# Narrow and wide expert turns interleaved in a two-layer decoder trunk, with another order of the layers' tasks

## The chip, the cores and the metric

The kernel runs on one NeuronCore of a Trainium2 chip. The metric is the device time of one execution in microseconds (us). TensorE is written PE here, VectorE DVE, ScalarE ACT, GpSimd POOL, SyncE SP; SP issues the loads.

## What is computed

The reference is a decoder trunk of two layers on 256 tokens of width 1024, in float32. Each layer has four mixer branches (S5, Mamba-2, retention, RG-LRU) merged by gates, a cross-attention on 256 memory tokens, and a feed-forward part. That part is a dense SwiGLU in layer 0 and eight experts in layer 1, of which each token takes two:

```python
def moe_swiglu(x, w_router, w1, w3, w2):
    logits = (t @ w_router).astype(jnp.float32)
    top_v, top_i = lax.top_k(logits, TOP_K)
    top_w = jax.nn.softmax(top_v, axis=-1)
    combine = jnp.einsum('tk,tke->te', top_w, jax.nn.one_hot(top_i, N_EXPERTS))
    out = combine[:, 0:1] * swiglu(t, w1[0], w3[0], w2[0])
    for e in range(1, N_EXPERTS):
        out = out + combine[:, e:e + 1] * swiglu(t, w1[e], w3[e], w2[e])
```

An expert has w1 and w3 of 1024 x 3584 and w2 of 3584 x 1024; the eight together are 352 MB of float32. A final RMSNorm ends the trunk.

## The kernel before

**The two layers.** Each projection is a `Job`: its weights come in loads of 512 KB, ACT and DVE split each into a high and a low float32r part (`whi`, `wlo`), and PE multiplies. Norms, scans, softmax and evacuations run as generators in lanes of the class `Loom`, which keeps a clock for each engine while the program is being written out and places a stage of a lane between two matmuls once it holds it to be ready. The table `ORDER` lists jobs and spawned tasks of both layers in the order in which they are written out (`0xa` is layer 0's cross-attention, `0xo0` a job of its output projection, `0ret` its retention). `LANES` holds two numbers for each lane: how early before its ready time a stage may be placed, and how far DVE and ACT may be behind. Each engine runs its instructions in the order written, so a matmul whose operand is late holds up everything behind it on PE.

**The experts** (`Trunk.experts`). The router counts the tokens of each expert, and `route` sorts the experts by count, the fullest first. There are eight turns; turn 0 is expert 0, and the number of the expert for each other turn is read from the sorted list when its loads are issued. A turn has a fixed number of places for tokens: the first five have 96 (`CP`), the last three 64 (`C0`). If an expert has more tokens than places, `overflow` runs the experts again for the rest.

A turn has seven blocks of 512 hidden columns. `up` multiplies eight loads (w1 and w3 side by side, `moe_w13`), `down` four (`moe_w2`); that is 12 loads of 512 KB, 84 for a turn and 672 in all. These weights are not split: PE multiplies raw float32. The matmuls for the first 64 places (`mm1`, 64 columns of the array for each half) and those for the other 32 (`mm2`, 32 columns for each quarter) are two passes over the same loads; a 64-place turn has only the first. The order is up(0), up(1), down(0), up(2), down(1) and so on across turns, so that `down` of a turn's last block stands behind `up` of the next turn's first.

`gather` picks the tokens of a turn (or of two turns at once, from turn 2 on) by matmuls with a 0/1 matrix `eg` into `xg`; it is started at a turn's fifth block for the next. `scatter` takes a finished turn back: ACT copies the sums from `py` to `ey` and rounds them to `eyh`, DVE makes the rest `eyl`, PE multiplies both by `eg`, and DVE adds the result into `h`.

**Loads.** SP issues them in the order of use. A load needs a free tile: 15 of three pools (`RAW`, `WHI`, `WLO`) and about 20 of the general pool (`rawm`), so some 35 loads, or 18 MB, may be ahead. A tile comes free when the last pass over it has run. `Stream.load` reckons with 1.43 ns for each element of a partition when it advances the clock of the loads.

Of the kernel before, what the change touches and what calls it, by code (L numbers as in the profile page):

```python
# [28 lines left out]
FF = 2816  # L29
FE = 3584  # L30
NE = 8
NB, CP, C0 = 5, 96, 64
AHEAD = 1
W1, W2, W3, W4 = 8, 4, 9, 4
SEC = dict(u=0, z=512, xbc=1024, dt=1792, q=1800, k=2312, v=2824, g=3336, xl=3848, gl=4360, gate=4872)
# [9 lines left out]


ORDER = """
0lru setup 0norm 0ret 0gl 0x 0run 0bc 0g 0ssd 0q 0build 0dt 0v 0u 0g1a 0g3b 0g3a 0z 0b3a 0b3b 0g1b 0b1a 0xa 0k 0g2a
0g2b 0mem 1run 0g0a 0glu 0b2a 0merge 0b1b 0g0b 0b2b 0xnorm 0b0b 0b0a 0K1 1build 0outa 0outb 0K0 0xq0 0V0 0xq1 1mem
0fnorm 0V1 1norm 0xo0 0xo1 1K1 0ffn 1lru 1K0 1x 1mem' 1ssd 1v 1dt 1bc 1ret 1u 1g3b 1gl 1xa 1q 1g3a 1k 1b3a 1b3b 1g  # L50
1g2b 1z 1g2a 1b2b 1g1b 1g1a 1b2a 1g0a 1merge 1b1a 1b1b 1g0b 1xnorm 1glu 1b0a 1b0b early 1outa 1outb 1V0 1xq0 1xq1 1V1
efnorm 1xo0 1xo1
"""


# [86 lines left out]
class Loom:  # L142
# [1 line left out]

    LANES = dict(norm=(0.2, 22.06), evac=(0.6, 1046.56), s5=(0.0, 3.12), q=(0.4, 3.12), a=(0.2, 2.0), b=(0.2, 3.12))

    BUSY = 5.5

# [118 lines left out]
class Stream:  # L269
# [12 lines left out]
    def load(self):  # L282
        k = self.k
        while len(self.loaded) < len(self.flat):
            j, (k0, nk) = self.flat[len(self.loaded)]
            w = j.w() if callable(j.w) else j.w
            src = w[k0 * P:(k0 + nk) * P, j.c0:j.c0 + j.n]

            pools = dict(raw=(k.wr, RAW))
            if j.raw and self.done >= self.parted:  # L290
                pools.update(whi=(k.wh, WHI), wlo=(k.wl, WLO))
            own = next((n for n, (_, bufs) in pools.items() if self.used[n] < bufs), None)
            if own:
                t = pools[own][0].tile([P, 1024], F32, tag=own, name=k.name("raw"))
                self.used[own] += 1
            elif k.loom.tiles + k.loom.want >= self.cap:
                break
            else:
                t = k.m("rawm")
            t = t[:, :nk * j.n]  # L300
            k.loom.clk["dma"] = max(k.loom.clk["dma"], k.loom.now) + nk * j.n * 1.43e-3
            k.nc.sync.eng.dma_start(t.rearrange("p (k n) -> p k n", k=nk), src.rearrange("(k p) n -> p k n", p=P))
            self.loaded.append((t, k.loom.clk["dma"] + 2.0, own))

# [111 lines left out]
class Trunk:  # L416
# [1373 lines left out]
    def moe(self, l, events):  # L1790
# [67 lines left out]

        def route():
            mp = self.cst  # L1860
            bef = self.m("bef")[:, 0:64].rearrange("p (i o) -> p i o", i=NE)
            nc.sync.dma_start(bef, a["before"].partition_broadcast(P))
            yield job.out
            sel, comb, slot = (mp.tile([P, 2, NE], F32, name=n) for n in ("sel2", "comb", "slot"))
            st.slot, st.comb, lg = slot, comb, st.lg.rearrange("p (t e) -> p t e", t=2)
# [37 lines left out]
            nc.vector.tensor_tensor(eq, eq, bef, op=ALU.mult)  # L1903
            nc.vector.tensor_tensor(oh, oh, eq, op=ALU.add)
            nc.vector.tensor_reduce(rk, oh, axis=AX.X, op=ALU.add)
            nc.vector.tensor_scalar(rk, rk, 1.0, None, op0=ALU.add)

            up = self.iota[:, 0:NE]
            nc.vector.tensor_tensor(oh, rk[:, None, :].to_broadcast(sh), up[:, :, None].to_broadcast(sh), op=ALU.is_equal)
            nc.vector.tensor_tensor(eq, oh, up[:, None, :].to_broadcast(sh), op=ALU.mult)  # L1910
            nc.vector.tensor_reduce(num, eq, axis=AX.X, op=ALU.add)
            nc.vector.tensor_scalar(num, num, -1.0, None, op0=ALU.add)
# [25 lines left out]

            yield 20.0
            last = sp[:, 0:2 * NE].rearrange("p (t e) -> p t e", t=2)  # L1940
            nc.vector.tensor_copy(last[:, :, :NB], st.slots[:, :, :NB])
            nc.vector.tensor_scalar(last[:, :, NB:], st.slots[:, :, NB:], CP / C0, None, op0=ALU.mult)
            ps = yield from self.bank()
            nc.tensor.transpose(ps[:2 * NE, 0:P], sp[:, 0:2 * NE], self.ident)
            yield
# [20 lines left out]
    def experts(self, st):  # L1966
# [7 lines left out]
        gathered = [[Event(), Event()] for _ in range(NE)]  # L1974
        done = [Event(), Event()]
        turns = [(0,), (1,), (2, 3), (4, 5), (6, 7)]
        cap = lambda e: CP if e < NB else C0

        def places(e):
            b_.xg.append(self.m(f"xg{e}").rearrange("p (d s) -> p d s", d=8))  # L1980
# [10 lines left out]
        def gather(es):  # L1991
# [5 lines left out]
                    places(e)  # L1997
            if es[0]:
                yield st.ordered
            i0, cp = es[0] % 4, cap(es[0])  # L2000
            G = b_.G[:, i0:i0 + n, :].rearrange("p i (t s) -> p i t s", t=2)
            for t in range(2):
                for i, e in enumerate(es):
# [30 lines left out]
        def scatter(e, py, halves, done=None):  # L2034
            S = b_.G[:, e % 4, :]
            if not b_.y:
                yield from self.room(3)
                b_.y += [self.m("ey"), self.m("eyh", F32R), self.m("eyl", F32R)]
                nc.gpsimd.memset(b_.y[0][CP:], 0.0)
            if e == NB:  # L2040
                nc.gpsimd.memset(b_.y[0][C0:CP], 0.0)
            y, yh, yl = b_.y
            yield st.weighted

            for c in halves:
                nc.scalar.copy(y[:C0, c * 512:c * 512 + 512], py[0][c * C0:c * C0 + C0, :])
                for q in range(2 * c, 2 * c + 2) if e < NB else ():
                    nc.scalar.copy(y[C0:CP, q * 256:q * 256 + 256], py[1][q * 32:q * 32 + 32, 0:256])
            o = slice(halves[0] * 512, halves[-1] * 512 + 512)
            if halves[-1]:  # L2050
                self.drop(len(py))
            yield
            nc.scalar.copy(yh[:, o], y[:, o])
            yield
            nc.vector.tensor_tensor(yl[:, o], y[:, o], f(yh)[:, o], op=ALU.subtract)
            yield
            for t in range(2):
                for c in halves:
                    o = slice(c * 512, c * 512 + 512)
                    ps = yield from self.bank()  # L2060
                    mm(ps, S[:, t * P:t * P + P], yh[:, o], start=True, stop=False)
                    mm(ps, S[:, t * P:t * P + P], yl[:, o], start=False, stop=True)
                    yield
                    hc = self.h[:, t, o]
                    nc.vector.scalar_tensor_tensor(hc, ps, st.comb[:, t, e:e + 1], hc, op0=ALU.mult, op1=ALU.add)
                    self.drop()
            if done:
                lm.signal(done)
# [10 lines left out]
        def up(e, b):  # L2079
# [13 lines left out]

            def ev(acc):
                nc.scalar.activation(t()[:, 0:256], acc[0][:, 0:256], AF.Silu)
                if e < NB:
                    nc.scalar.activation(t()[:, 256:384], acc[1][:, 0:128], AF.Silu)
                yield
                nc.vector.tensor_tensor(t()[:, 0:256], t()[:, 0:256], acc[0][:, 256:512], op=ALU.mult)
                if e < NB:  # L2100
                    nc.vector.tensor_tensor(t()[:, 256:384], t()[:, 256:384], acc[1][:, 128:256], op=ALU.mult)
                yield

                pt = yield from self.bank()
                n = 3 if e < NB else 2
                for j in range(n):
                    nc.tensor.transpose(pt[:, j * P:j * P + P], t()[:, j * P:j * P + P], self.ident)
                yield
                nc.vector.tensor_copy(b_.h[i][:, :n * P], pt[:, :n * P])
                self.drop()  # L2110

            need = lambda k: (gathered[e][k // 4],)
            j = Job(lambda: a["moe_w13"][turn(e), b], 0, 1024, 8, 1 + (e < NB), mm1, ev, need)
            j.raw = True
            if e < NB:
                j.more = mm2
            return j

        def down(e, b, done, py):
            def start():  # L2120
                if not py:
                    n = 1 + (e < NB)
                    lm.until(lambda: lm.side >= n)
                    lm.side -= n
                    py.extend(self.sidep.tile([P, 512], F32, tag="side", name=self.name("py")) for _ in range(n))
# [16 lines left out]
            jw = dict(need=lambda k: (done,), start=start)  # L2142
            if e < NE - 1 or b < nb - 1:
                jobs = [Job(w, 0, 1024, 4, 0, mm1, **jw)]
                if e < NB:
                    jobs[0].more, jobs[0].front = mm2, True
            else:
                jobs = [Job(w, c * 512, 512, 4, 0, lambda *x, c=c: mm1(*x, halves=(c,)), **jw) for c in range(2)]
# [22 lines left out]
    def overflow(self, st):  # L2171

        nc, raw = self.nc, self.raw
        last = raw.values_load(st.most[0:1, 0:1], min_val=0, max_val=2 * T)
        st.again = True
        for n in (CP, 2 * CP):
            with self.tc.If(last > n):
                nc.vector.tensor_scalar(st.slots[:, :, :NB], st.slots[:, :, :NB], float(CP), None, op0=ALU.subtract)
                nc.vector.tensor_scalar(st.slots[:, :, NB:], st.slots[:, :, NB:], float(C0), None, op0=ALU.subtract)
                self.stream(self.experts(st), more=True)  # L2180


# [94 lines left out]
def layout(inp):  # L2277
# [37 lines left out]
    for i, nm in enumerate(("lru_wa", "lru_wx")):  # L2315
# [8 lines left out]
                                 g["norm_final"][None, :]], axis=0),  # L2324
        "pp": z, "lam": np.stack(lam, axis=1).transpose(2, 1, 0, 3).reshape(P, -1), "s5bc": np.stack(s5, axis=3), "lruw": lw.reshape(NL, P, 2, 4, P),
        "kst": kst, "decay": decay, "freq": freq,
        "before": np.tril(np.ones((NE, NE), np.float32), -1)[None],
        **{n: g[n] for n in ("w_in", "b_gate", "s5_w_glu", "w_branch", "w_out", "xa_wq", "xa_wk", "xa_wv", "xa_wo",
                             "ffn_w1", "ffn_w3", "ffn_w2")},
        "moe_router": g["moe_router"][0], "moe_w2": g["moe_w2"][0],  # L2330
# [19 lines left out]
```

## Time and profile before

| | |
|---|---|
| median of 3 runs | 2095.37 us (2089.89 to 2096.30) |
| the profiled execution, its own time | 2091.97 us |
| its span, first to last instruction | 2090.1 us |
| busy: PE, DVE, ACT, POOL | 1984.1, 952.5, 648.0, 135.9 us |
| mean granted PE clock, as a share of 2.4 GHz | 0.974 |
| moved from HBM | 535.57 MB, 257 GB/s over the span |

The page divides the span into 40 slices of 52 us. PE is at nine tenths or more in most, and lower in the first, in two early ones and in the last three. The memory traffic is different: 122 to 263 GB/s in the two layers (to slice 22), 315 to 394 in slices 23 to 34, and 409 without change in slices 36 to 39. The chain that ended last is 79% PE and 9% DMA.

### The profile page before, as it was taken

What the parts mean: (1) busy time and instruction counts of PE and PEld (TensorE: products, weight loads), DVE (VectorE), ACT (ScalarE), POOL (GpSimd) and SP (SyncE); (2) the same over time, 40 slices, a digit from 0 to 9 for tenths busy, and PEclk for the clock granted to TensorE, in tenths of its full rate; (3) what the DMA queues carried; (4) which work ended last, traced back from release to release, by engine and by line L of the source; (5) the groups of instructions that cost most, each with busy time, mean ns of one, the idle gap of its engine ahead of it and who ended that gap; (6) DMA issues with size and microseconds to landing.
All of it is one profiled execution on the core that took longest, in us unless ns stands there. A gap on an engine that the chain in (4) does not pass through costs nothing.

```text
span 2090.1 us, 33394 instructions
## 1 busy us (share of the span) xinstructions
PE 1984.1 (95%) x12937; PEld 1275.4 (61%) x12937; DVE 952.5 (46%) x1750; ACT 648.0 (31%) x1041; POOL 135.9 (7%) x282
## 2 busy tenths in 40 slices
PE   7999889999999999999999999999999999999885
PEld 7878677898888998887798344434434343333211
DVE  5888988857555689788655101111010100110102
ACT  4755434545444484444453001010010000010001
POOL 6840005000000000000000000000000000000000
PEclk9999899999999999999999999999999999999998
DMA  6544345546665555445746989988989899999994
GB/s 224 166 141 137 122 134 169 177 145 213 185 193 185 183 179 153 149 125 174 263 161 240 386 345 370 352 346 315 394 315 352 332 371 394 402 409 409 409 409 188
DMA packets 194434, 539.00 MB, mean 258 GB/s; under 512 B 18442, under 2 KB 23562, under 8 KB 194258
## 3 DMA queue, kind: packets, MB, share of 16 engines
q1 hardware_dynamic: 194258, 536.69, 70.9%
q8 instruction: 106, 1.74, 0.3%
q14 instruction: 70, 0.57, 0.1%
HBM read 535.57 MB, written 1.05 MB: 257 GB/s over the span
## 4 chain that ended last, share of the span: by engine, by line
PE 79%; DMA 9%; DVE 4%; POOL 3%; ACT 2%; issue 1%; SPq 0%; DVEq 0%; ACTq 0%; POOLq 0%
PE acc L132 59%; PE py L132 10%; PE ps L132 10%; DMA rawm<-moe_w 5%; DMA raw<-moe_w 2%; DVE wlo L132 1%; POOL tbt L132 1%; ACT ey L132 1%; POOL scr L132 1%; DMA s5z<-s5bc 1%; DVE s5z L132 0%; ACT whi L132 0%; DVE s5s L132 0%; POOL sp_e L132 0%; DVE eyl L132 0%
## 5 line engine op out<-in xcount | busy, mean ns | idle before, releaser
L132 DVE TENSOR_TENSOR wlo<-raw,whi 128x1024 fp32r<-128x1024 f32 (+2 forms) x311 | 372.3, 1215 | 118.0 <-PE acc L132 60.9
L132 ACT ACTIVATE whi<-raw 128x1024 fp32r<-128x1024 f32 (+2 forms) x311 | 322.4, 1052 | 225.0 <-PE acc L132 177.7
L132 DVE TENSOR_TENSOR eht<-eht,acc 128x256 f32<-128x256 f32 x91 | 33.7, 370 | 667.4 <-ACT eht L132 667.4
L132 PE MATMUL acc<-rawm,xg 128*32 128x256 f32 (+1 forms) x2308 | 321.3, 482 | 6.3 <-DMA rawm<-moe_w 6.2
L132 ACT ACTIVATE eht<-acc 128x256 f32<-128x256 f32 x91 | 31.2, 343 | 758.1 <-PE acc L132 758.1
L132 PE MATMUL acc<-whi,xh 128*128 128x512 f32 (+1 forms) x640 | 254.8, 398 | 0.1
L132 PE MATMUL acc<-wlo,xh 128*128 128x512 f32 (+1 forms) x640 | 247.2, 386 | 3.4 <-DVE wlo L132 3.3
L132 PE MATMUL acc<-whi,xl 128*128 128x512 f32 (+1 forms) x640 | 246.6, 385 | 0.0
L132 PE MATMUL acc<-raw,xg 128*32 128x256 f32 (+1 forms) x1724 | 239.0, 479 | 4.0 <-DMA raw<-moe_w 3.8
L132 PEld LDWEIGHTS acc<-rawm,xg 128*32 128x32 f32 (+1 forms) x2308 | 109.1, 122 | 199.0 <-issue 129.0
L132 PE MATMUL acc<-xh,whi 128*128 128x256 f32 (+1 forms) x632 | 181.9, 288 | 1.4 <-ACT whi L132 1.2
L132 PE MATMUL acc<-xh,wlo 128*128 128x256 f32 (+1 forms) x632 | 179.5, 284 | 3.6 <-DVE wlo L132 3.6
L132 PE MATMUL acc<-xl,whi 128*128 128x256 f32 (+1 forms) x632 | 179.6, 284 | 0.6 <-DVE xl L132 0.4
L132 PE MATMUL py<-rawm,eh 128*32 128x256 f32 (+1 forms) x1140 | 165.7, 478 | 4.2 <-DMA rawm<-moe_w 4.1
L132 PEld LDWEIGHTS acc<-raw,xg 128*32 128x32 f32 (+1 forms) x1724 | 82.1, 122 | 142.5 <-issue 88.9
L132 PEld LDWEIGHTS acc<-whi,xh 128*128 128x128 f32 x640 | 120.7, 189 | 28.6 <-issue 5.7
L132 PEld LDWEIGHTS acc<-wlo,xh 128*128 128x128 f32 x640 | 120.7, 189 | 26.5 <-DVE wlo L132 5.1
L132 PEld LDWEIGHTS acc<-whi,xl 128*128 128x128 f32 x640 | 120.6, 188 | 24.3 <-DVE xl L132 0.2
L132 PE MATMUL py<-raw,eh 128*32 128x256 f32 (+1 forms) x876 | 126.0, 477 | 1.2 <-DMA raw<-moe_w 1.2
L132 PEld LDWEIGHTS acc<-xh,wlo 128*128 128x128 f32 (+1 forms) x632 | 119.3, 189 | 4.4 <-DVE wlo L132 3.8
L132 PEld LDWEIGHTS acc<-xh,whi 128*128 128x128 f32 (+1 forms) x632 | 119.2, 189 | 3.8 <-ACT whi L132 1.5
L132 PEld LDWEIGHTS acc<-xl,whi 128*128 128x128 f32 (+1 forms) x632 | 119.2, 189 | 2.7 <-DVE xl L132 1.5
(399 smaller groups left out, 2304.6 us busy)
## 6 DMA issues: line engine op xcount, KB each, us to landing
rawm<-moe_w SPq DMA_DIRECT2D x384, 512.0 KB, 10.1
raw<-moe_w SPq DMA_DIRECT2D x288, 512.0 KB, 9.5
raw<-w_in SPq DMA_DIRECT2D x136, 512.0 KB, 3.8
raw<-ffn_w SPq DMA_DIRECT2D x66, 512.0 KB, 4.1
raw<-w_branch SPq DMA_DIRECT2D x32, 512.0 KB, 3.5
raw<-xa_wk SPq DMA_DIRECT2D x16, 512.0 KB, 4.2
raw<-w_out SPq DMA_DIRECT2D x16, 512.0 KB, 4.0
raw<-xa_wq SPq DMA_DIRECT2D x13, 512.0 KB, 3.4
```

Of the source, the lines that this page charges most:

```text
L132: return fn(out, *a, **k)
```

## The change

The changed kernel is written out in another order at four places.

- `RANKS` gives each turn the rank of its expert by count: turns 0 to 7 take ranks 0, 5, 1, 2, 6, 3, 7, 4. Ranks 0 to 4 have 96 places and 5 to 7 have 64, so the turns have 96, 64, 96, 96, 64, 96, 64, 96 places. `route` looks the rank up in a small table that comes with `before` instead of using the turn's number, and where the turns were compared with `NB`, `big(e)` now stands. A pair is gathered at the wider of its two widths. The two jobs of the last `down` have only `mm1`, as before, though the last turn now has 96 places.
- `scatter` waits 0.3 us more in the loom's clock before its first copy, and both halves of a row of tokens are now multiplied into two banks before DVE adds them.
- The reckoned price of a load of 1024 columns (the experts' alone) is 1.26 ns instead of 1.43.
- `ORDER` and `LANES` have other entries.

The two layers have the same 5915 matmuls before and after (by kind and size); those of the experts change with the widths.

```diff
-NB, CP, C0 = 5, 96, 64
+CP, C0 = 96, 64
+RANKS = (0, 5, 1, 2, 6, 3, 7, 4)
+PLACES = tuple(CP if r < 5 else C0 for r in RANKS)
...
 ORDER = """
-0lru setup 0norm 0ret 0gl 0x 0run 0bc 0g 0ssd 0q 0build 0dt 0v 0u 0g1a 0g3b 0g3a 0z 0b3a 0b3b 0g1b 0b1a 0xa 0k 0g2a
+0lru 0norm setup 0ssd 0run 0ret 0x 0bc 0gl 0u 1run 0v 0build 0dt 0g 0g3b 0g1a 0b3b 0q 0g3a 0b3a 0z 0b1a 0k 0g0b 0mem
...
-    LANES = dict(norm=(0.2, 22.06), evac=(0.6, 1046.56), s5=(0.0, 3.12), q=(0.4, 3.12), a=(0.2, 2.0), b=(0.2, 3.12))
+    LANES = dict(norm=(1.0, 41.7), evac=(0.6, 1290.03), s5=(0.4, 3.82), q=(0.4, 3.27), a=(0.6, 2.0), b=(0.2, 3.12))
...
-            k.loom.clk["dma"] = max(k.loom.clk["dma"], k.loom.now) + nk * j.n * 1.43e-3
+            k.loom.clk["dma"] = max(k.loom.clk["dma"], k.loom.now) + nk * j.n * (1.26e-3 if j.n == 1024 else 1.43e-3)
...
-            nc.vector.tensor_tensor(oh, rk[:, None, :].to_broadcast(sh), up[:, :, None].to_broadcast(sh), op=ALU.is_equal)
+            nc.vector.tensor_tensor(oh, rk[:, None, :].to_broadcast(sh), ranks[:, :, None].to_broadcast(sh), op=ALU.is_equal)
...
-        cap = lambda e: CP if e < NB else C0
+        big = lambda e: PLACES[e] > C0
...
-            i0, cp = es[0] % 4, cap(es[0])
+            i0, cp = es[0] % 4, max(PLACES[e] for e in es)
...
             yield st.weighted
+            yield 0.3
...
             for t in range(2):
-                for c in halves:
+                bs = (yield from self.two_banks()) if len(halves) > 1 else [(yield from self.bank())]
+                for ps, c in zip(bs, halves):
                     o = slice(c * 512, c * 512 + 512)
-                    ps = yield from self.bank()
                     mm(ps, S[:, t * P:t * P + P], yh[:, o], start=True, stop=False)
                     mm(ps, S[:, t * P:t * P + P], yl[:, o], start=False, stop=True)
-                    yield
-                    hc = self.h[:, t, o]
+                yield
+                for ps, c in zip(bs, halves):
+                    hc = self.h[:, t, c * 512:c * 512 + 512]
                     nc.vector.scalar_tensor_tensor(hc, ps, st.comb[:, t, e:e + 1], hc, op0=ALU.mult, op1=ALU.add)
...
-            j = Job(lambda: a["moe_w13"][turn(e), b], 0, 1024, 8, 1 + (e < NB), mm1, ev, need)
+            j = Job(lambda: a["moe_w13"][turn(e), b], 0, 1024, 8, 1 + big(e), mm1, ev, need)
             j.raw = True
-            if e < NB:
+            if big(e):
                 j.more = mm2
```

**A scatter on PE.** Before, at the scatter of turn 1 (`py` is the last `down` of the finished turn, `ps<-eyh,eg` the scatter, `acc` the next block's `up`):

```order
6058 L132 MATMUL py_11814<-rawm_12291,eh_10702 64x512 x2
6059 L132 MATMUL py_11814<-rawm_12297,eh_10702 64x512 x2
6060 L132 MATMUL ps_12596<-eyh_11851,eg_10705 128x512
6061 L132 MATMUL ps_12596<-eyl_11852,eg_10705 128x512
6062 L132 MATMUL ps_12600<-eyh_11851,eg_10705 128x512
6063 L132 MATMUL ps_12600<-eyl_11852,eg_10705 128x512
6064 L132 MATMUL acc_12605<-rawm_12303,xg_1992_12212 64x512 x2
6065 L132 MATMUL ps_12610<-eyh_11851,eg_10705 128x512
```

After, at the scatter of turn 2:

```order
6158 L135 MATMUL py_12313<-rawm_12715,eh_10702 64x512 x2
6159 L135 MATMUL acc_13008<-rawm_12721,xg_1767_10704 64x512 x2
6160 L135 MATMUL acc_13008<-rawm_12727,xg_1767_10704 64x512 x2
6161 L135 MATMUL acc_13008<-rawm_12733,xg_1767_10704 64x512 x2
6162 L135 MATMUL acc_13008<-raw_12739,xg_1767_10704 64x512 x2
6163 L135 MATMUL acc_13008<-raw_12745,xg_1767_10704 64x512 x2
6164 L135 MATMUL acc_13008<-rawm_12751,xg_1767_10704 64x512 x2
6165 L135 MATMUL ps_13030<-eyh_11721,eg_10705 128x512
6166 L135 MATMUL ps_13030<-eyl_11722,eg_10705 128x512
```

The scatter stood straight behind the last `down`; now five or six loads' worth of the next `up` stand between. Before, the scatters of turns 1 to 6 stood so, and that of turn 0 already had five loads' worth ahead of it; after, all seven that a later turn follows have five or more.

**Layer 0's cross-attention on PE.** Before (`xk,xq` are the scores, `kst,xp` the transposes of the softmax, `acc` a projection), rows 2027 to 2033, with 18 more `acc` rows behind them ahead of the transposes:

```order
2027 L132 MATMUL ps_4408<-xk_4159,xq_4370 128x256 x4
2028 L132 MATMUL acc_4373<-whi_4298,xh_3220 128x512
2029 L132 MATMUL acc_4373<-wlo_4334,xh_3220 128x512
2030 L132 MATMUL acc_4373<-whi_4298,xl_3221 128x512
2031 L132 MATMUL acc_4374<-whi_4298,xh_3220 128x512
2032 L132 MATMUL acc_4374<-wlo_4334,xh_3220 128x512
2033 L132 MATMUL acc_4374<-whi_4298,xl_3221 128x512
```

After:

```order
2216 L135 MATMUL acc_4544<-xh_4216,wlo_4590 128x256
2217 L135 MATMUL ps_4727<-xk_4383,xq_4534 128x256 x4
2218 L135 MATMUL ps_4744<-kst,xp_4388 128x128
2219 L135 MATMUL ps_4744<-kst,xp_4389 128x128
2220 L135 MATMUL ps_4744<-kst,xp_4388 128x128
```

The 24 `acc` rows between the scores and the transposes are gone.

**Layer 0's retention on PE.** Before (`kst,ry` are the transposes of its normed result):

```order
1397 L132 MATMUL acc_2986<-s5yh_3035,whi_2919 128x256
1398 L132 MATMUL acc_2986<-s5yl_3036,whi_2919 128x256
1399 L132 MATMUL acc_2986<-s5yh_3035,wlo_2942 128x256
1400 L132 MATMUL ps_3180<-kst,ry_3040 128x128 x4
1401 L132 MATMUL ps_3189<-kst,ry_3040 128x128 x4
1402 L132 MATMUL acc_3162<-whi_2944,yrh_3178 128x512
```

After:

```order
1403 L135 MATMUL acc_3189<-whi_3104,xh_127 128x512
1404 L135 MATMUL acc_3189<-wlo_3128,xh_127 128x512
1405 L135 MATMUL acc_3189<-whi_3104,xl_128 128x512
1406 L135 MATMUL ps_3198<-kst,ry_2962 128x128 x4
1407 L135 MATMUL acc_3188<-whi_3104,xh_127 128x512
```

Ahead of these transposes there are now 56 `acc` rows of 128x512 more than the S5 projection that stood there before, and the second group of four comes 61 rows later.

## Rows read from the trace of the kernel before

**Rows 1.** Busy time by stage: stretch, engines (us and count), PE clock, DMA share, GB/s.
```profile
0.00:1150.00 1150.00, 1106.95 (x6534) 942.48 (x6536) 847.28 (x1515) 576.74 (x860) 134.03 (x280) 0.98 0.54 174
1150.00:1768.00 618.00, 604.61 (x5265) 251.83 (x5263) 64.48 (x146) 47.08 (x126) 0.95 (x1) 0.98 0.92 355
1768.00:2058.00 290.00, 262.75 (x1119) 77.91 (x1116) 31.16 (x61) 18.52 (x44) 0.94 (x1) 0.96 1.02 407
```
**Rows 2.** What SP waited for, 1420 to 1520 and 1900 to 2040: us, times, longest.
```profile
SPq L302 <- PE acc L132: 54.9, 27, 14.3
...
SPq L302 <- DMA rawm<-moe_w: 47.2, 62, 1.5
```
**Rows 3.** Chain of waits in blocks of 96-place turns, a scatter and a gather: start, us, what.
```profile
1262.48 3.58 PE py L132 x16
...
1278.73 3.58 PE py L132 x16
...
1313.78 3.58 PE py L132 x16
...
1346.27 3.58 PE py L132 x16
...
1368.13 3.58 PE py L132 x16
...
1400.62 3.61 PE py L132 x16
...
1426.09 3.58 PE py L132 x16
```
**Rows 4.** Chain of waits in 64-place turns.
```profile
1793.40 2.73 PE py L132 x12
1796.13 6.89 PE acc L132 x32
...
1804.38 2.73 PE py L132 x12
```
**Rows 5.** Timeline around the scatter of turn 1: start, us, engine, what, [idle before, releaser].
```profile
1403.61 0.60 PE L132 MATMUL py<-rawm,eh 128*64 128x512 f32 x2
1408.11 0.79 PE L132 MATMUL ps<-eyh,eg 128*128 128x512 f32 x1 [3.90 <-ACT eyh L132]
1409.37 0.79 PE L132 MATMUL ps<-eyl,eg 128*128 128x512 f32 x1 [0.47 <-DVE eyl L132]
```
**Rows 6.** As group 1, short stretches: two scatters, then two with fast loads.
```profile
1300.00:1350.00 50.00, 50.00 (x446) 20.90 (x444) 9.00 (x19) 1.99 (x6) 0.00 (x0) 1.00 0.90 340
1396.00:1420.00 24.00, 19.63 (x139) 7.66 (x127) 4.99 (x7) 3.93 (x8) 0.00 (x0) 0.86 0.71 272
...
1180.00:1230.00 50.00, 50.00 (x453) 21.05 (x450) 4.20 (x11) 1.98 (x6) 0.00 (x0) 1.00 1.01 395
...
1450.00:1453.00 3.00, 3.00 (x22) 0.92 (x22) 0.00 (x0) 0.17 (x1) 0.00 (x0) 1.00 1.05 419
```
**Rows 7.** End of the chain of waits.
```profile
2047.24 10.29 DMA rawm<-moe_w
...
2064.34 3.59 PE py L132 x8
```
**Rows 8.** What PE waited for, 0 to 1150: us, times, longest.
```profile
PE acc L132 <- DVE wlo L132: 6.9, 3, 3.6
PE ps L132 <- DMA kst<-kst: 6.5, 1, 6.5
PE ps L132 <- DVE ry L132: 5.0, 2, 4.2
PE ps L132 <- issue: 4.9, 1, 4.9
```
**Rows 9.** Timeline of layer 0's softmax, PE and DVE.
```profile
432.73 1.89 PE L132 MATMUL ps<-xk,xq 128*128 128x256 f32 x8
...
438.00 0.69 DVE L132 TENSOR_TENSOR xp<-xp,xsm 128x512 f32<-128x512 f32 x1
```

More of the change, by code (lines that the diff above doesn't have):

```diff
@@ L47 @@
 ORDER = """
-0lru setup 0norm 0ret 0gl 0x 0run 0bc 0g 0ssd 0q 0build 0dt 0v 0u 0g1a 0g3b 0g3a 0z 0b3a 0b3b 0g1b 0b1a 0xa 0k 0g2a
[L49 to L52, printed above, removed]
+0lru 0norm setup 0ssd 0run 0ret 0x 0bc 0gl 0u 1run 0v 0build 0dt 0g 0g3b 0g1a 0b3b 0q 0g3a 0b3a 0z 0b1a 0k 0g0b 0mem
+0xa 0g2b 0g2a 0merge 0glu 0g1b 0g0a 0b2b 0K1 0b2a 0b1b 0V1 0xnorm 1mem 0fnorm 1build 0b0b 0b0a 0V0 0outb 0outa 0K0
+0xq0 1norm 0xq1 0xo1 0xo0 1K1 0ffn 1K0 1lru 1ssd 1x 1ret 1dt 1v 1mem' 1bc 1u 1merge 1g3b 1gl 1q 1xa 1xnorm 1g3a 1k
+1b3b 1b3a 1g 1g2b 1z 1g2a 1b2b 1b2a 1g0b 1g1b 1V1 1g1a 1glu 1g0a 1b0a 1b1a 1b0b early 1b1b 1outb 1outa 1V0 1xq0 efnorm
+1xq1 1xo0 1xo1
 """
@@ L1860, in route @@
             mp = self.cst
-            bef = self.m("bef")[:, 0:64].rearrange("p (i o) -> p i o", i=NE)
+            bef = self.m("bef")[:, 0:72].rearrange("p (i o) -> p i o", o=NE)
             nc.sync.dma_start(bef, a["before"].partition_broadcast(P))
+            bef, ranks = bef[:, 0:NE, :], bef[:, NE, :]
             yield job.out
@@ L1905, in route @@
             nc.vector.tensor_reduce(rk, oh, axis=AX.X, op=ALU.add)
-            nc.vector.tensor_scalar(rk, rk, 1.0, None, op0=ALU.add)
             up = self.iota[:, 0:NE]
-            nc.vector.tensor_tensor(oh, rk[:, None, :].to_broadcast(sh), up[:, :, None].to_broadcast(sh), op=ALU.is_equal)
+            nc.vector.tensor_tensor(oh, rk[:, None, :].to_broadcast(sh), ranks[:, :, None].to_broadcast(sh), op=ALU.is_equal)
             nc.vector.tensor_tensor(eq, oh, up[:, None, :].to_broadcast(sh), op=ALU.mult)
@@ L1940, in route @@
             last = sp[:, 0:2 * NE].rearrange("p (t e) -> p t e", t=2)
-            nc.vector.tensor_copy(last[:, :, :NB], st.slots[:, :, :NB])
-            nc.vector.tensor_scalar(last[:, :, NB:], st.slots[:, :, NB:], CP / C0, None, op0=ALU.mult)
+            nc.vector.tensor_copy(last, st.slots)
+            for e in range(NE):
+                if PLACES[e] < CP:
+                    nc.vector.tensor_scalar(last[:, :, e:e + 1], st.slots[:, :, e:e + 1], CP / C0, None, op0=ALU.mult)
             ps = yield from self.bank()
@@ L2039, in scatter @@
                 nc.gpsimd.memset(b_.y[0][CP:], 0.0)
-            if e == NB:
+            if e and big(e - 1) and not big(e):
                 nc.gpsimd.memset(b_.y[0][C0:CP], 0.0)
@@ L2043, in scatter @@
             yield st.weighted
+            yield 0.3
             for c in halves:
                 nc.scalar.copy(y[:C0, c * 512:c * 512 + 512], py[0][c * C0:c * C0 + C0, :])
-                for q in range(2 * c, 2 * c + 2) if e < NB else ():
+                for q in range(2 * c, 2 * c + 2) if big(e) else ():
                     nc.scalar.copy(y[C0:CP, q * 256:q * 256 + 256], py[1][q * 32:q * 32 + 32, 0:256])
@@ L2099, in ev @@
                 nc.vector.tensor_tensor(t()[:, 0:256], t()[:, 0:256], acc[0][:, 256:512], op=ALU.mult)
-                if e < NB:
+                if big(e):
                     nc.vector.tensor_tensor(t()[:, 256:384], t()[:, 256:384], acc[1][:, 128:256], op=ALU.mult)
@@ L2104, in ev @@
                 pt = yield from self.bank()
-                n = 3 if e < NB else 2
+                n = 3 if big(e) else 2
                 for j in range(n):
@@ L2112, in up @@
             need = lambda k: (gathered[e][k // 4],)
-            j = Job(lambda: a["moe_w13"][turn(e), b], 0, 1024, 8, 1 + (e < NB), mm1, ev, need)
+            j = Job(lambda: a["moe_w13"][turn(e), b], 0, 1024, 8, 1 + big(e), mm1, ev, need)
             j.raw = True
-            if e < NB:
+            if big(e):
                 j.more = mm2
@@ L2121, in start @@
                 if not py:
-                    n = 1 + (e < NB)
+                    n = 1 + big(e)
                     lm.until(lambda: lm.side >= n)
@@ L2144, in down @@
                 jobs = [Job(w, 0, 1024, 4, 0, mm1, **jw)]
-                if e < NB:
+                if big(e):
                     jobs[0].more, jobs[0].front = mm2, True
@@ L2177, in overflow @@
             with self.tc.If(last > n):
-                nc.vector.tensor_scalar(st.slots[:, :, :NB], st.slots[:, :, :NB], float(CP), None, op0=ALU.subtract)
-                nc.vector.tensor_scalar(st.slots[:, :, NB:], st.slots[:, :, NB:], float(C0), None, op0=ALU.subtract)
+                for e in range(NE):
+                    v = st.slots[:, :, e:e + 1]
+                    nc.vector.tensor_scalar(v, v, float(PLACES[e]), None, op0=ALU.subtract)
                 self.stream(self.experts(st), more=True)
@@ L2326, in layout @@
         "kst": kst, "decay": decay, "freq": freq,
-        "before": np.tril(np.ones((NE, NE), np.float32), -1)[None],
+        "before": np.concatenate([np.tril(np.ones((NE, NE), np.float32), -1), np.array(RANKS, np.float32)[None]])[None],
         **{n: g[n] for n in ("w_in", "b_gate", "s5_w_glu", "w_branch", "w_out", "xa_wq", "xa_wk", "xa_wv", "xa_wo",
```

## The prediction

> **What bounds the kernel now.** I read the page's slices first, then busy time by stage, then the waits and the chain inside the experts. To 1150 us the two layers run, and PE is busy 1107 of 1150 us [rows 1]: PE bounds them, and the memory is at less than half its rate. From 1150 to 1768 us the five 96-place turns run. PE is busy 605 of 618 us there, loads arrive at 355 GB/s, and what SP waits for is a tile that PE has not yet freed [rows 1, 2]. From 1768 to 2058 us the three 64-place turns run. Now loads arrive at 407 GB/s, PE has gaps, and SP waits for its own transfers [rows 1, 2]; the last load ends the stage [rows 7]. So the same stage is bound by PE first and by the loads afterwards, and in its first part the loads stand still for lack of room.
>
> The lengths behind this: between the last matmuls of two blocks of a 96-place turn lie 1278.73 - 1262.48 = 16.25 us of PE, in a 64-place turn 1804.38 - 1793.40 = 10.98 us [rows 3, 4]. A load is 0.524 MB, which at 409 GB/s (the page's last slices) takes 1.28 us; twelve take 15.4 us. A wide block needs PE longer than its loads, a narrow one needs its loads longer than PE. That the loads keep up their rate beside a busy PE is seen where a burst of tiles has come free: 419 GB/s with PE busy for all of 3 us [rows 6].
>
> **The change, part by part.** I work out when PE ends its last `down` if it never waits for a load, then what the loads add, then the two ends of the program. Turn 0 ends its last `down` at 1278.73 + 3.58 = 1282.3 us now [rows 3].
>
> *Interleaving.* The first `up` of turn 1 lies before that point and loses its second pass: a narrow block is 5.27 us shorter than a wide one, and `up` has 8 of the 12 loads, so 3.5 us. After it come 49 blocks, 28 wide (turns 2, 3, 5, 7) and 21 narrow: 28 x 16.25 + 21 x 10.98 = 685.6 us. The first `up` has been done already (6.9 us [rows 4]), and the last `down` has no second pass (a third of 5.27, 1.8 us).
>
> *Gathers.* Three of pairs are left, and one shows as 1368.13 - 1346.27 - 16.25 = 5.6 us [rows 3]. They add 16.8 us. That the last pair is now gathered wider is within this, since I price it as a wide one.
>
> *Scatters.* The scatter of turn 1 lengthens its block to 25.47 us, so it costs 9.2 us: PE waits 3.9 us for `eyh` and 0.5 for `eyl`, and then its clock is down [rows 3, 5]. The clock shows as 0.86 of 2.4 GHz in the 24 us around it, and as 1.00 around the scatter of turn 0 [rows 6], ahead of which five loads' worth of `up` stand: two blocks with that scatter take 1313.78 - 1278.73 = 35.05 us [rows 3], 2.55 more than 32.5. In the new order every scatter has such cover. Five loads' worth are 6.89 x 5/8 = 4.3 us [rows 4], and the waits without cover end 3.9 us (`eyh`) and about 5.2 us (`eyl`) behind the last `down` [rows 5]; the scatters with five loads ahead are those of narrow turns, which have two of six copies instead of six, and the wide ones have six loads, 5.2 us. I take 2.55 us for each of seven: 17.9. With no cover each would be 9.2.
>
> Sum: 1282.3 - 3.5 + 685.6 - 6.9 - 1.8 + 16.8 + 17.9 = 1990.4 us, against 2064.34 + 3.59 = 2067.9 now [rows 7].
>
> *Loads.* From 1150 to 2058 us 618 x 355 + 290 x 407 GB/s = 337 MB arrive [rows 1]. At 409 GB/s these take 825 us: done at 1975, earlier than PE. But room is limited. Some 35 loads can be ahead, 45 us of transfer. A turn needs 84 x 1.28 = 107.7 us of loads. PE takes 116 to 122 us for a wide turn (7 x 16.25, a scatter, perhaps a gather), so the lead grows by 9 to 14 us, and 79 to 85 us for a narrow one, so it shrinks by 23 to 28. From 40 us after turn 0 the lead goes 17, 26, 40, 12, 26, -2 over turns 1 to 6; from 35, it ends at -7. PE then waits a few us in turn 6; I add 8, since tiles come free in bursts. Last `down`: 1998.
>
> *The end.* From the last `down` to the end are 2090.1 - 2067.9 = 22.2 us. The new order sends both halves' scatters behind the last `down`, which I price at 1 us. Span 2021.6; the experts give 68 us.
>
> *The layers.* The work is the same, only its order differs. PE stands idle 43 us there [rows 1], of which 6.5 us are the first constants [rows 8]. Two places show both signs. The wait of 5.0 us for retention's `ry` [rows 8] goes, as 13 us of other matmuls now stand ahead. Layer 0's softmax loses its cover: from the end of the scores at 434.6 us to the end of `xp` at 438.7 lie 4.1 us [rows 9], now spent idle, and some more where the values follow at once. As I can't price the rest, the ends are a gain of 25 us (two thirds of the idle time) and a loss of as much; I take 0, between the two that I can see.
>
> *The rest.* One DVE instruction fewer in `route`, six small ones more 20 us later: DVE is busy 64 of 618 us there [rows 1], nothing. `LANES` and the reckoned price of a load only place instructions.
>
> The profiled execution took 2091.97 us, so the sum is about 2025 in its own terms (68 less, with 1 for clock lost where PE waits in turn 6). It lies 3.4 us below the median of the runs; I add 2 and say **2027 us**, 3.3% below the median.
>
> **Rivals.**
>
> *The layers gain too.* If two thirds of their idle time goes, 2027 - 25 = 2002. For it: waits of 6.9, 5.0 and 4.9 us that cover could end [rows 8]. Against: the softmax. Chance 0.11.
>
> *The layers lose.* 2052 by the same measure. For it: the softmax. Chance 0.08.
>
> *Loads run short.* Beside PE they arrive at 395 GB/s in the best 50 us [rows 6]. If 390 is all that they reach, 337 MB take 865 us, the last arrives at 2015, and with about 4 us for the `down` behind it and the end the program takes some 2045. Against: 419 GB/s [rows 6]. Chance 0.07.
>
> *The scatters stay uncovered* (the change doesn't do what it says). Seven times 6.65 us more is 47, of which the 8 us of waiting are absorbed: about 2065. Against: the order. Chance 0.05.
>
> *Loads are the bound from the start to the end.* If the stage's mean of today, 337 MB in 908 us or 372 GB/s, is a ceiling, the last load arrives at 2058 as now, and the time is 2092 to 2095: no change. Against: 290 us at 407 GB/s [rows 1]. Chance 0.03. The Trainium skill has such a rule (HBM Reference, Specifications): some 358 GB/s for a core, half of what a pair shares, though a core alone gets about 425. By the 358 the change would be worth nothing, and an estimate from it puts the 352 MB at 984 us. The trace disagrees with 407 to 419, and fits the second figure.
>
> *Slower than before.* The new order opens waits in the layers as it does in layer 0's softmax, at 4 us each with a stretch of low clock behind it, some 5 to 6 us in all by what a scatter shows beyond its matmuls [rows 3, 5]. It decides when they eat the 68 us, at about 13 such places more than now; with 16 it would be 2027 + 88 = 2115. For it: one such place is there. Against: another went, and the waits of before that I read are few and short. Chance 0.04.
>
> **How the numbers follow.** The forecast has 0.62. The range reaches to the gain and the loss in the layers and takes in short loads: 2003 to 2052. Outside lie the uncovered scatters, no change, slower, and the edges, under 0.2. A measurement can tell about 0.3%, 6 us, from no change. Faster: 0.62 + 0.11 + 0.08 + 0.07 + 0.05 = 0.93; same 0.03; slower 0.04.
>
> **What would show it.** Right: loads near 400 GB/s through the whole expert stage, with no part at 409 without change at the end; waits for `eyh` gone; blocks still 16.25 and 10.98 us; the last `down` about 70 us nearer to the start of the experts than now. Wrong: PE idle in the layers well over or under 43 us; waits of PE for loads in turns 1 or 4; blocks longer than now.

## The result and the profile after

The changed kernel takes 2039.8 us, median of 4 runs (2036.21 to 2044.53); the kernel before took 2095.15 on the same chip. The ratio is 0.9742, with a 95% interval from 0.9716 to 0.9768: 2.6% faster. The forecast, 2027 us, lay 12.8 us lower; the range from 2003 to 2052 holds the result. The profiled execution has a span of 2038.7 us, where the sum gave 2021.6: 17.1 us are to be found.

The GB/s line of the page's 40 slices, after:

```profile
GB/s 240 145 149 140 93 139 203 183 197 114 197 176 196 168 207 153 160 142 148 165 258 156 324 393 346 409 409 409 408 408 389 401 409 408 409 408 409 407 405 94
```

Before, 409 stood only in the last slices; now it stands, within 1 or 2, from slice 26 to slice 38 with one dip. The prediction wanted to see "near 400" and no long stretch at 409 at the end: the loads have less margin than it said. Busy time by turn shows the same (as [rows 1]; the stretches are about those from one turn's last `down` to the next, turn 0 first):

```profile
1153.00:1286.00 133.00, 133.00 (x1120) 54.31 (x1121) 12.15 (x38) 12.14 (x30) 0.95 (x1) 0.98 0.96 373
1286.00:1370.00 84.00, 83.50 (x441) 30.67 (x439) 11.08 (x24) 6.14 (x19) 0.95 (x1) 1.00 1.03 409
1370.00:1490.00 120.00, 120.00 (x1059) 49.46 (x1057) 12.83 (x26) 10.06 (x24) 0.00 (x0) 1.00 1.03 408
1490.00:1607.00 117.00, 117.00 (x1006) 49.22 (x1003) 13.18 (x29) 9.75 (x29) 0.00 (x0) 1.00 1.00 396
1607.00:1689.00 82.00, 81.51 (x423) 28.06 (x421) 10.30 (x20) 5.89 (x14) 0.95 (x1) 1.00 1.03 409
1689.00:1806.00 117.00, 117.00 (x1006) 49.33 (x1004) 13.19 (x29) 8.32 (x25) 0.00 (x0) 1.00 1.03 408
1806.00:1907.00 101.00, 92.04 (x432) 25.37 (x429) 10.30 (x20) 8.05 (x18) 0.95 (x1) 1.00 1.03 409
1907.00:2012.00 105.00, 104.23 (x900) 42.84 (x897) 12.25 (x24) 6.32 (x17) 0.00 (x0) 1.00 0.88 346
```

Turns 1 and 4 (64 places) take 84 and 82 us, turn 6 (also 64 places) 101. It is the only stretch in which PE is idle for more than 1 us (9 of 101), and the loads run at 409 there. The chain of waits says the same: from 1791.76 to 1896 us it leaves PE for ten transfers in a row. The prediction's rival "Loads run short" (390 beside PE) falls by the row of turn 2: 408 with PE busy for all of 120 us.

```profile
1687.39 4.29 PE acc L135 x20
...
1791.76 10.10 DMA rawm<-moe_w
...
1801.98 10.84 DMA raw<-moe_w
...
1885.28 10.81 DMA rawm<-moe_w
...
1905.02 4.29 PE acc L135 x20
```

Turns 4 and 6 have the same work. Turn 4's last `down` ends 82.7 us after turn 3's (1604.71 to 1687.39), turn 6's ends at 1905.02, 99.5 us after turn 5's. So the loads cost 16.8 us in turn 6.

The scatter of turn 2, as in the chain (compare [rows 3, 5]):

```profile
1483.01 3.58 PE py L135 x16
1486.60 5.15 PE acc L135 x24
1491.74 2.04 PE ps L135 x8
...
1501.45 3.58 PE py L135 x16
...
1517.70 3.58 PE py L135 x16
```

Six loads' worth of `up` stand between `py` and `ps`, and the eight matmuls of the scatter follow one another without a wait in 2.04 us: the block of the scatter takes 1501.45 - 1483.01 = 18.44 us, the next one 16.25. The wait for `eyh` has gone at all seven turns that another follows; one is left, behind the last. What PE waited for, 1150 to 2039 us:

```profile
PE acc L135 <- DMA rawm<-moe_w: 5.1, 18, 0.9
PE ps L135 <- ACT eyh L135: 3.8, 1, 3.8
PE acc L135 <- DMA raw<-moe_w: 1.8, 8, 0.3
```

What SP waited for answers to [rows 2]: from 1480 to 1610 us, in turn 3, and from 1690 to 1925, in turns 5 and 6.

```profile
SPq L305 <- DMA rawm<-moe_w: 35.0, 48, 1.0
...
SPq L305 <- PE acc L135: 14.7, 19, 5.1
```

```profile
SPq L305 <- DMA rawm<-moe_w: 72.2, 96, 1.5
...
SPq L305 <- PE acc L135: 6.9, 25, 0.4
```

In turn 3 it waits for its own transfers most of the time, but also up to 5.1 us at once for PE to free a tile: the room is full at times. Later it waits for its own transfers almost alone.

### The profile page after: what moved, and what is told of

The parts are those of the page before. It is cut to its first block, busy times and chain, and to the rows that moved or that the text cites. A ratio compares the mean times of both kernels' runs of the same rounds, so it can differ in the third digit from the quotient of the medians.

```text
span 2038.7 us, 33351 instructions
## 1 busy us (share of the span) xinstructions
PE 1958.3 (96%) x12905; PEld 1275.2 (63%) x12905; DVE 948.3 (47%) x1751; ACT 649.3 (32%) x1041; POOL 133.2 (7%) x284
## 4 chain that ended last, share of the span: by engine, by line
PE 71%; DMA 5%; ACT 1%; DVE 1%; issue 0%; SPq 0%; ACTq 0%; DVEq 0%
PE acc L135 52%; PE py L135 11%; PE ps L135 8%; DMA raw<-moe_w 3%; DMA rawm<-moe_w 3%; DMA rdt<-decay 0%; DVE eht L135 0%; ACT eht L135 0%; DVE n L135 0%; ACT xp L135 0%; ACT ey L135 0%; DVE rs_t L135 0%; DVE h L135 0%; ACT nw L135 0%; DVE rs L135 0%
## 5 line engine op out<-in xcount | busy, mean ns | idle before, releaser
L135 DVE TENSOR_TENSOR wlo<-raw,whi 128x1024 fp32r<-128x1024 f32 (+1 forms) x312 | 374.5, 1219 | 135.4 <-PE acc L135 67.4
L135 ACT ACTIVATE whi<-raw 128x1024 fp32r<-128x1024 f32 (+1 forms) x312 | 323.8, 1054 | 248.1 <-PE acc L135 211.1
L135 DVE TENSOR_TENSOR eht<-eht,acc 128x256 f32<-128x256 f32 (+1 forms) x91 | 33.7, 370 | 635.0 <-ACT eht L135 635.0
L135 PE MATMUL acc<-rawm,xg 128*64 128x512 f32 (+1 forms) x2304 | 315.2, 477 | 5.2 <-DMA rawm<-moe_w 5.1
L135 ACT ACTIVATE eht<-acc 128x256 f32<-128x256 f32 (+1 forms) x91 | 31.2, 343 | 699.8 <-PE acc L135 699.8
L135 PEld LDWEIGHTS acc<-rawm,xg 128*64 128x64 f32 (+1 forms) x2304 | 109.5, 122 | 193.2 <-issue 134.2
L135 PE MATMUL py<-rawm,eh 128*32 128x256 f32 (+1 forms) x1136 | 160.8, 477 | 1.8 <-DMA rawm<-moe_w 1.0
## 6 DMA issues: line engine op xcount, KB each, us to landing
rawm<-moe_w SPq DMA_DIRECT2D x382, 512.0 KB, 10.1
raw<-moe_w SPq DMA_DIRECT2D x290, 512.0 KB, 10.1
```

Source lines behind the costliest of these rows:

```text
L135: return fn(out, *a, **k)
```

## The experiments

In the table, the start is the first matmul of the experts in the chain of the profiled execution, the experts' time runs from there to the end of the last `down`, and the end is what is left of the span.

| run | ratio to before, interval | start | experts | end |
|---|---|---|---|---|
| before | 1 | 1149.7 | 918.2 | 22.2 |
| the change | 0.9742, 0.9716 to 0.9768 | 1153.0 | 858.6 | 27.0 |
| the change again | 0.9742, 0.9724 to 0.9761 | 1149.4 | 858.6 | 26.8 |
| e1, turns alone | 0.9844, 0.9825 to 0.9862 | 1147.8 | 881.0 | 23.5 |
| e2, layers undone | 0.9706, 0.9685 to 0.9727 | 1151.1 | 858.9 | 25.9 |
| e3, turns sorted | 0.9893, 0.9870 to 0.9916 | 1147.7 | 894.3 | 24.0 |
| e5, price undone | 0.9738, 0.9706 to 0.9770 | 1146.9 | 860.6 | 26.8 |
| e6, scatter undone | 0.9831, 0.9805 to 0.9857 | 1157.7 | 877.6 | 23.7 |
| e7, last turn narrow | 0.9688, 0.9669 to 0.9707 | 1156.6 | 849.9 | 25.9 |
| e8, four tiles less | 0.9778, 0.9763 to 0.9793 | 1151.9 | 862.4 | 24.9 |
| e9, e7 with old layers | 0.9678, 0.9655 to 0.9702 | 1150.2 | 849.5 | 25.3 |
| e11, eight tiles less | 0.9790, 0.9758 to 0.9821 | 1154.3 | 868.8 | 24.8 |

The change gave the same experts' time twice, while the start moved by 3.6 us. So the experts' time tells versions apart far better than the whole time; each is still one profiled execution.

**Turns alone (e1).** `before` with the new turns and nothing else:

```diff
+RANKS = (0, 5, 1, 2, 6, 3, 7, 4)
+PLACES = tuple(CP if r < 5 else C0 for r in RANKS)
```

> The kernel before with only the interleaved turns (ranks 0, 5, 1, 2, 6, 3, 7, 4); ORDER, LANES, the scatter and the reckoned price of a load as before. In this order at most one load's worth of the next up stands between a last down and its scatter. Theory (interleaving lets the loads run through, covered scatters come on top, the layers' order gives nothing): experts start at 1149.6 us as before; seven scatters cost 9.2 us again instead of 2.04, 50 us, of which some 17 us are absorbed because the changed kernel's PE waits that long for loads: some 33 us above the changed kernel less 3.4 us of layers, about 2070 us. Rival A (the interleaving does it all, the scatters wait in time that the loads need anyway): 2036 us. Rival B (the scatters do it all): at least 2085 us.

The run took 2059.5 us, between the theory and rival A: the interleaving alone takes 37 us from the experts.

**Turns sorted (e3).** The change with the old order of turns:

```diff
-RANKS = (0, 5, 1, 2, 6, 3, 7, 4)
+RANKS = (0, 1, 2, 3, 4, 5, 6, 7)
```

> The changed kernel with the turns in sorted order (five of 96 places, then three of 64); the scatters stay covered by three to six loads' worth of up. Theory: in the five wide turns the loads stand still for lack of room and PE gains what the scatters lost (four times 7.2 us), in the three narrow ones the loads bound it at 409 GB/s: 24 to 28 us above the changed kernel, 2064 to 2068 us, with PE waiting for loads in the last 250 us. Rival A (the covered scatters are the whole gain): 2040 us. Rival B (the interleaving is the whole gain): 2095 us.

The run took 2069.6 us, just above the theory; both rivals fall. Covered scatters without the interleaving take 24 us from the experts. Alone, the two parts give 37 and 24 us, together 60, so they nearly add up. Busy time of this run (as above; the last wide turn ends at 1752 us):

```profile
1607.00:1689.00 82.00, 82.00 (x739) 34.20 (x737) 10.28 (x20) 6.95 (x17) 0.00 (x0) 1.00 0.96 375
1689.00:1806.00 117.00, 116.67 (x787) 45.10 (x785) 12.76 (x28) 9.04 (x26) 0.94 (x1) 1.00 1.01 400
1806.00:1907.00 101.00, 93.20 (x392) 25.32 (x388) 10.72 (x21) 6.16 (x15) 0.00 (x0) 1.00 1.03 409
1907.00:2012.00 105.00, 90.35 (x346) 19.30 (x344) 9.03 (x17) 4.51 (x9) 0.00 (x0) 1.00 1.03 409
```

First PE is full and the loads run at 375, then the loads are full and PE waits, as before the change.

**Scatter undone (e6).** The change with the old `scatter`:

```diff
-            yield 0.3
...
-                bs = (yield from self.two_banks()) if len(halves) > 1 else [(yield from self.bank())]
-                for ps, c in zip(bs, halves):
+                for c in halves:
...
+                    ps = yield from self.bank()
```

> The changed kernel with the scatter as before (no 0.3 us, one bank at a time); at most one load's worth of up stands ahead of each scatter. Theory: each scatter costs 9.2 us again, 50 us together, of which up to 17 us are absorbed in the waits for loads: 2066 to 2075 us, with waits of PE for eyh of 3 to 4 us at seven places and fewer for loads. Rival A (two banks alone make scatters cheap, the cover adds nothing): with neither it would be the same 50 us less nothing absorbed, 2090 us. Rival B (the waits are absorbed altogether): 2040 us.

The run took 2060.2 us, 20 more than the change, below the theory's 2066. Both rivals fall. Its waits:

```profile
PE ps L135 <- ACT eyh L135: 20.7, 8, 3.9
PE ps L135 <- DVE eyl L135: 4.1, 8, 0.8
```

The waits for loads are gone altogether, and turn 6 takes 90.4 us instead of 99.5, though its own block with a scatter is longer: the 16.8 us that the change loses to loads there are won back, and the scatters lose more than that in all. By turns, against the change: turns 3 and 4, which hold a wide turn's scatter, are 7.1 and 7.6 us longer, but turns 2 and 5, which hold a narrow one's, only 3.1 (turn 2 takes 119.0 us instead of 115.9). The theory had the price of wide ones for all; narrow ones have two copies by ACT where wide ones have six, and in the 25 us around one the clock stays at 1.00, where it is 0.85 around a wide one:

```profile
1700.00:1725.00 25.00, 22.64 (x187) 9.01 (x187) 5.73 (x9) 3.25 (x6) 0.00 (x0) 1.00 1.03 409
1822.00:1845.00 23.00, 18.64 (x94) 6.65 (x92) 5.04 (x7) 4.04 (x8) 0.94 (x1) 0.85 1.03 409
```

This run takes back both parts of the new scatter, the 0.3 us and the two banks; which of them brings the cover was not tried.

**Less room (e8, e11).** The change with four, and with eight, tiles less for the experts' loads:

```diff
-            self.cur.cap = MB
+            self.cur.cap = MB - 4
```

> The changed kernel with four tiles less in the general pool that the experts' loads use, so that four loads less can be ahead. Theory (the lead after turn 3 is what the last narrow turn lives on): PE waits 4 x 1.28 = 5.1 us longer in turn 6, about 5 us above the changed kernel. Rival (the rate of the loads is the bound, the room is not): within 1 us of the changed kernel.

> The changed kernel with eight tiles less in the pool that the experts' loads use. Theory (the room decides; with four less, turn 4 became 2.9 us longer and the whole stretch 3.8 us, so the lead after turn 3 was 22 loads in the changed kernel): four more cost their full 5.1 us in turn 4, so that it takes some 90.7 us instead of 82.7, and turn 6 stays at about 100: 867 us from the first expert matmul to the last down instead of 858.6. Rival (the loss with four less was by chance): 858 to 863 us.

With four less the run took 2044.4 us beside 2036.9 for the change on the same chip, with eight less 2049.8. The experts take 3.8 and 10.2 us longer, so both rivals fall. With four less, turn 4 takes 85.6 us instead of 82.7 and turn 6 100.1 instead of 99.5; with eight less, turn 4 takes some 91.8 us (from turn 2's end and the 118.1 us of a turn 3 without waits to 1698.0). Its row has PE busy for 86.9 of them:

```profile
1606.16:1698.00 91.84, 86.91 (x425) 26.38 (x423) 10.29 (x20) 6.62 (x15) 0.95 (x1) 1.00 1.03 409
```

The room decides. For e8 the turn was named wrongly: the missing loads are felt in the first narrow turn that starts with too few, turn 4.

**Last turn narrow (e7), and with the old layers (e9).**

```diff
-RANKS = (0, 5, 1, 2, 6, 3, 7, 4)
+RANKS = (0, 5, 1, 2, 6, 3, 4, 7)
```

> The changed kernel with the ranks of the last two turns exchanged: 0, 5, 1, 2, 6, 3, 4, 7, so the places are 96, 64, 96, 96, 64, 96, 96, 64 and two wide turns stand ahead of the last narrow one. Theory (a landed lead of at most 24 to 30 loads; a narrow turn uses up some 20 of them, a wide one wins back some 8 to 11): after turns 1 to 7 the lead is about 5, 16, 27, 3, 14, 25 and 1 loads, PE waits no more in turn 6, 17 us of waits fall to some 5 us at the end: 8 to 12 us below the changed kernel, 2028 to 2032 us. Rival A (the loads' rate from start to end bounds it, wherever the waits show): the same time as the changed kernel within 3 us. Rival B (the waits were bursts, not a lead run out): the same, with the waits still between 1800 and 1900 us.

> The run with the last turn narrow, and ORDER and LANES as in the kernel before. Theory 1 (the new order of the layers costs some 3 us): 3 to 5 us below that run. Theory 2 (the difference of 4.6 us between the changed kernel and the run with the layers undone is the spread of executions; the start of the experts lies between 1148 and 1158 us with either order): within 2 us of that run, and the order of the layers gives nothing that can be told.

The runs took 2026.0 and 2027.1 us: e7 takes 0.9945 of the change's time on the same chip (0.9688 / 0.9742), 8.7 us less in the experts. Both beat the changed kernel. In e7's busy time (turn 4; turns 5 and 6; turn 7) the gap of turn 6 is gone and a shorter one stands at the end:

```profile
1607.00:1690.00 83.00, 82.51 (x427) 28.43 (x425) 10.29 (x20) 6.62 (x15) 0.95 (x1) 1.00 1.03 409
1690.00:1924.00 234.00, 234.00 (x2047) 97.73 (x2045) 25.99 (x55) 17.66 (x47) 0.00 (x0) 1.00 1.03 408
1924.00:2007.00 83.00, 78.22 (x330) 23.79 (x327) 9.72 (x18) 7.16 (x15) 1.89 (x2) 1.00 0.94 370
```

Both rivals to e7 fall: two wide turns ahead of the narrow one restore what it lives on. e9 lies within 2 us of e7, as theory 2 said, and shows no gain or loss by the layers' order.

**Layers undone (e2), price undone (e5), the change again (e10).** e2 has `ORDER` and `LANES` of `before`, e5 its price, e10 is the change itself.

```diff
-    LANES = dict(norm=(1.0, 41.7), evac=(0.6, 1290.03), s5=(0.4, 3.82), q=(0.4, 3.27), a=(0.6, 2.0), b=(0.2, 3.12))
+    LANES = dict(norm=(0.2, 22.06), evac=(0.6, 1046.56), s5=(0.0, 3.12), q=(0.4, 3.12), a=(0.2, 2.0), b=(0.2, 3.12))
...
-nk * j.n * (1.26e-3 if j.n == 1024 else 1.43e-3)
+nk * j.n * 1.43e-3
```

> The changed kernel with ORDER and LANES as before. Theory: the layers' new order costs 3.4 us (the experts start at 1153.0 instead of 1149.6) and LANES does nothing in the experts: start 1149.6, turns as in the changed kernel, about 2036 us. Rival A (the new LANES also lengthened the end behind the last down from 23.2 to 27.0 us): 2032.5 us, with 23 us behind the last down. Rival B (the new order of the layers helps in the experts, by what it leaves loaded ahead): 2040 us or above.

> The changed kernel with the reckoned price of an experts' load back at 1.43 ns. The scatters then have four loads' worth of cover in narrow turns and six in wide ones instead of five and six. Theory (the price only places instructions): from the first expert matmul to the last down 858.6 us as in the changed kernel, within 1 us; any other time comes from the layers. Rival (the price sets how the small stages stand among the matmuls, and a wrong one costs a little in every block): blocks of 16.4 instead of 16.25 us in some turns, as in the run with the turns alone, and 4 to 6 us more in this stretch.

> The changed kernel itself, to have it beside the other three on one chip. Expected: 2036 to 2044 us as in its runs so far, and, for the spread of the layers, another start of the experts than 1153.0 us by up to 5 us.

The runs took 2035.2, 2037.6 and 2036.9 us: no difference that a measurement can tell. Rivals A and B of e2 both fall (its end is 25.9 us, not 23, and its experts take 858.9), but its theory, that the new order costs 3.4 us, isn't shown either: its experts start at 1151.1, within the spread of both orders (below). e5 is 2.0 us longer in the experts, between theory and rival: some of its blocks take 16.38 us instead of 16.25, which is too little to show in the whole time.

## Why the prediction was right, and where it was short

*The mechanism* held: wide turns bound by PE and narrow ones by the loads, side by side they fill each other's gaps. Blocks are 16.25 and 10.97 us as before [rows 3, 4] (a narrow one from 1626.11 to 1637.08). The experts went from 918.2 to 858.6 us.

*The sum without waits* gave 711.6 us from turn 0's last `down` (1282.3 less 3.5) to the last one; the trace shows 2011.67 - 1282.52 - 16.8 = 712.4. The scatter term was 2.55 us each; the block above with one is 2.2 us longer than the next. That "in the new order every scatter has such cover" held; the rival without cover said 2065, and e6 measured 2060. Its price of 9.2 us was right for wide turns alone.

*The step that failed* is the size of the lead: "Some 35 loads can be ahead, 45 us of transfer", and from it 40 us after turn 3 (35 by its lower start). With 1.28 us for a load, turn 4 needs 84 and gets 82.7 / 1.28 = 64.6 while it runs, so it lives on 19.4 that have landed before. It ran without a wait, so at least so many were there; with four tiles less it was 2.9 us, or 2.3 loads, short. So some 19.4 - 2.3 + 4 = 21 loads had landed after turn 3: 27 us.

The trace of the change can also be counted. These are the experts' loads that SP had issued when turn 3's last `down` ended (1604.71 us; how many, KB each, us from issue to landing):

```profile
rawm<-moe_w SPq DMA_DIRECT2D x212, 512.0 KB, 10.1
raw<-moe_w SPq DMA_DIRECT2D x163, 512.0 KB, 10.1
```

PE had used 344 of these 375 (84 for each of four turns, 8 for the first `up` of turn 4), so 31 were ahead. Of them 8 had been issued in the last 10.1 us and were still on their way: a load lands every 1.28 us, but takes 10.1 from issue to landing. So 23 had landed, 29 us. The other 4 of the 35 tiles held the loads of the last `down` itself. Tiles being filled and tiles in use had been counted as lead.

The ledger from 27 or 29 us, with the turns' own times: turn 4 leaves 2 to 4 us (counted as before, 3 loads), turn 5 (118.1 us) adds 10.4, turn 6 takes 25: short by 10 to 13, where 16.8 were measured. The prediction allowed 8. Of the rest, some 2.6 us are 2 landed loads that are left when turn 6 ends; where the last 2 to 4 us lie is open. That a tile less is a load less was tried (e8, e11), and so was that two wide turns ahead of the last narrow one take most of its waits away (e7).

The Trainium skill (HBM Reference, Specifications) gives some 358 GB/s as a core's half of what a pair shares and 425 for a core alone. The 408 to 409 of this trace, held over 504 of the 621 us of turns 1 to 6, disagree with the first as a limit here and lie 4% below the second.

*The end* was "which I price at 1 us"; it is 3.8 us longer than that price (27.0 for 22.2 + 1). The start of it was misread. Before, a scatter stood between the two halves of the last `down`:

```profile
2057.66 3.63 PE py L132 x8
...
2063.38 0.96 PE ps L132 x3
2064.34 3.59 PE py L132 x8
```

The second half starts 3.0 us behind the end of the first (2061.3); counting from its end [rows 7] left that wait out. Now the two halves follow within 0.7 us, and the wait comes behind them. In the chain of the change:

```profile
2001.11 7.07 PE py L135 x26
...
2008.88 2.79 PE py L135 x6
2011.67 0.67 PE ps L135 x2
...
2013.69 0.84 ACT n L135 x3
...
2014.56 0.58 ACT ey L135
...
2017.32 1.48 PE ps L135 x3
```

From the first half's end to the end are 28.8 us before (2090.1 - 2061.3), 30.5 in the change (2038.7 - 2008.2) and 31.1 in e6, with the old scatter (2059.0 - 2027.9). Counted so, the end is 1.7 us longer than before, near the price of 1, and the new scatter is not what lengthens it. ACT now squares what the first half has finished, for the norm, before it copies the second half.

*The layers* were taken at 0. The change's trace starts the experts 3.3 us later, but that is one execution: with the new order they start between 1146.9 and 1157.7 us in eight traces, with the old between 1147.8 and 1151.1 in four. Both signs that were named are in the waits: the one for `ry` [rows 8] is gone, and a wait for `xp` is there. What PE waited for, 0 to 1150 us, after:

```profile
PE ps L135 <- issue: 10.7, 4, 4.2
PE ps L135 <- DMA kst<-kst: 6.2, 1, 6.2
...
PE ps L135 <- ACT dz L135: 5.1, 2, 4.2
PE acc L135 <- DVE xl L135: 3.7, 3, 2.5
...
PE ps L135 <- ACT xp L135: 2.3, 1, 2.3
```

The softmax was priced at 4.1 us and waits 2.3. Longer waits for `dz` (5.1 us) and `xl` (3.7) and under "issue" (10.7, before 4.9; a wait that the profile puts down to nothing) make up for those that went. Idle time is 1153.0 - 1107.3 = 45.7 us, where 43 were foreseen.

Together: 3.3 (start) + 1.2 (work on PE: 0.8 in the 712.4 and 0.4 from the start to turn 0's end) + 8.8 (loads, 16.8 less 8) + 3.8 (end) = 17.1 us. All four have one sign, so nothing was hit by errors that cancel; but the start could as well have come out early: in e5, with the same order, it is 2.8 us ahead of the kernel before.

## What to carry to other kernels

Where one kind of step is bound by compute and another by loads, put them in turn, and check by a ledger of what is loaded ahead that each load-bound step starts with enough. Count as ahead only what has landed: tiles being filled or still being read are taken, and the measured need of one step (its loads less those that land while it runs) sizes the lead better than a count of buffers. Time the stage that was changed apart from the rest, when an earlier stage varies from one execution to the next.

## What had not been expected

The layers vary by more than the effects that were looked for, in part through the clock. The same instructions in the same order, first in the change and then in e6:

```profile
200.00:300.00 100.00, 86.13 (x535) 68.89 (x536) 91.04 (x199) 40.72 (x72) 1.47 (x3) 0.88 0.35 108
300.00:400.00 100.00, 100.00 (x535) 83.78 (x534) 80.66 (x134) 52.30 (x74) 25.94 (x52) 1.00 0.57 191
```

```profile
200.00:300.00 100.00, 86.06 (x496) 68.60 (x497) 86.67 (x189) 38.98 (x70) 1.47 (x3) 0.82 0.34 107
300.00:400.00 100.00, 100.00 (x542) 85.03 (x542) 77.51 (x132) 49.13 (x70) 24.31 (x52) 0.97 0.54 180
```

With 14 us of PE idle in both, the granted clock is 0.88 in one and 0.82 in the other, and 0.97 instead of 1.00 in the stretch behind. Layer 0's attention scores start at 456.6 and 463.1 us. Five of the six other traces with this order show 0.88, and one, e7, 0.81; e6 and e7 are the two latest starts of the experts. The clock of this stretch isn't all of the spread: with 0.88 they still start anywhere from 1146.9 to 1154.3 us. What decides it was not tried.
